# Modulation products of two k tiles at once in the first layer, with zero products ahead of them and the growth of the Fourier input moved ahead of both

## The chip, the cores and the metric

One core of a Trainium2 chip runs the whole program. The metric is the device time of one execution in microseconds; lower is better. The engines named below are TensorE (PE in the rows; PEld is its weight load), VectorE (DVE), ScalarE (ACT), GpSimd (POOL) and SyncE (SP), which issues most of the loads.

## The reference, cut to what matters

Two layers of an encoder over two requests with shared weights (512 and 256 tokens, width 1024). What matters here is the beginning of the first layer:

```
mod = silu(c) @ w_ada[l] + b_ada[l]                 # c: one row for each request
sh1, sc1, gt1, sh2, sc2, gt2 = split(mod, 6)        # 1024 columns each
h = rms_norm(x, g_mix_pre[l]) * (1 + sc1) + sh1     # 768 tokens x 1024
z = h @ w_in[l]                                     # u_f is 512 of its columns (Fourier branch)
```

The modulation shift `sh1` and scale `sc1` need 2 x 1024 columns of `w_ada[0]`, 8 MB. Until one tile of 128 of these columns is known, the same 128 columns of `h` can't be formed, and `h @ w_in` can't use them. All of it is float32 in effect: `h` and the weights of `w_in` are split into a high and a low part, and each product of the two is three matmuls.

## The kernel before

The first stage of layer 0 is written by hand in `start()`. The 1024 columns of `h` are eight k tiles of 128. For each k tile there are four steps' worth of work:

- the loads `ws[k, i]`: the shift and scale columns of `w_ada[0]` that belong to tile k, two blocks of 512 KB, each loaded by two DMAs of 256 KB whose rows in HBM are 128 columns (512 bytes) long;
- `ada(k)` (line 1725): `mod_mm` multiplies them with silu(c). These are eight float32 products with 256 moving columns that use 32 columns of the array each; four of them (one for each 32-column strip) run side by side. ScalarE then copies the sums out of PSUM (line 1732);
- `fin(k)` (line 1737): tiny products with `sel` (line 1744) turn the sums into columns, VectorE adds the bias and the gain (lines 292 and 294), ScalarE makes the high part of `h` (line 1750), VectorE the low part (lines 1751 and 1753) and the reversed copies (line 685), which the symmetric Fourier transform needs;
- `grow(k)` (line 1757): twelve matmuls of 128x512 (lines 1765 to 1767) add tile k's part of `u = h @ w_in[:, fourier]` for the four token tiles of the first request. The third matmul of a token tile needs the low part; token tiles 2 and 3 read the reversed copies.

The weights of `w_in` for `grow` are `uw[0]` to `uw[3]`, each for two k tiles. `keep(n)` (line 1782) issues n products of a constant with a block of zeros, whose sums nobody reads. `norm(4)`, `norm(5)` and `h_step` (lines 1700 and 433) bring in the second request: its two token tiles are normalized, transposed (line 398) and scaled. After `grow(7)` come the steps `us[2]`, the same growth for the second request (lines 770 to 772).

The order of the work: steps are a list, and `run()` emits them one by one. Up to step 43 (`FIXED`, which is `grow(6)` in both versions) every engine does its instructions in the order in which they are written; behind that a scheduler decides. Before a step is emitted, `run()` issues the loads that come next, as far as the step's `hold` allows (five loaded blocks not yet used, here), so SP's queue has the loads in the order in which the steps need them. A load waits until its block is free and until the eighth load before it has landed.

Before the change the steps interleave: `fin(k + 1)`, `ada(k + 2)`, `grow(k)`. So while VectorE and ScalarE work on `fin(k + 1)`, TensorE has `ada(k + 2)` and `grow(k)` to do.

Of the kernel before, what the change touches and what calls it, by code (L numbers as in the profile page):

```python
# [11 lines left out]
F32 = mybir.dt.float32  # L12
F32R = mybir.dt.float32r
AF = mybir.ActivationFunctionType
# [3 lines left out]
D = 1024  # L18
# [23 lines left out]

HP = 50
FIXED = 43
KEEP = [0, 0, 0, 2, 3, 0]
SPIN = [17, 14]


# [19 lines left out]
def encoder_trunk(ctx, tc, a, consts, y_prompt, y_sample):  # L68
    nc = tc.nc
# [11 lines left out]
    def nm(s):  # L81
        uid[0] += 1
        return f"{s}_{uid[0]}"

    def row(dt=F32):
        return rp.tile([128, 768], dt, tag="r", name=nm("r"))

    def double(dt=F32, shape=(128, 1536)):
        return dbl.tile(list(shape), dt, tag="d", name=nm("d"))
# [8 lines left out]
    def blk(dt=F32, shape=(128, 1024)):  # L98
        blocks.append(wp.tile(list(shape), dt, tag="w", name=nm("w")))
        return blocks[-1]  # L100
# [6 lines left out]
    def small(n=2):  # L107
        return sp.tile([128, n], F32, tag=f"s{n}", name=nm("s"))

    def bank():  # L110
        return pp.tile([128, 512], F32, tag="ps", name=nm("ps"))

    def f(ap):
        return ap.bitcast(F32)
# [6 lines left out]
    sel = cp.tile([128, 2], F32, name="sel")  # L121
# [85 lines left out]
    def rstd(sums, n=1):  # L207

        v, r = small(1), small(1)
        if len(sums) > 1:  # L210
            nc.gpsimd.tensor_scalar(out=v, in0=sums[0], scalar1=EPS, scalar2=sums[1], op0=ALU.add, op1=ALU.add)
        else:
            nc.gpsimd.tensor_scalar(out=v, in0=sums[0], scalar1=1.0 / n, scalar2=EPS, op0=ALU.mult, op1=ALU.add)
        nc.gpsimd.tensor_tensor(out=r, in0=v, in1=neg_half, op=ALU.pow)
        return r

    def mean_square(out, x, n, acc):
        nc.scalar.activation(out=out, in_=x, func=AF.Square, scale=float(n) ** -0.5, accum_out=acc)  # L218
# [56 lines left out]
    def mod_mm(ps, srcs):  # L275

        for s in range(2):
            for j in range(4):
                k = s * 4 + j
                nc.tensor.matmul(ps[32 * j:32 * j + 32, :], c32[:, k, :], srcs[k], start=(s == 0), stop=(s == 1),  # L280
                                 tile_position=(0, 32 * j))
# [1408 lines left out]
    def start(uw, us, S):  # L1690

        out = []
        mp, pu, xl, xT = {}, [], {}, []
        ws = {}
        for k in range(8):
            for i in range(2):
                parts = [(s * 512, 512, a["w_ada"][0][i * 512:(i + 1) * 512, s * D + k * 128:s * D + (k + 1) * 128].rearrange(
                    "(j p) c -> p j c", p=128), ("p (j c) -> p j c", dict(j=4))) for s in range(2)]
                ws[k, i] = Weight(parts, 1024, split=False)

        def norm(t):
            def emit():
                x = xl.pop(t)
                jk, ss = blk(F32), small(1)
                mean_square(jk, x, D, ss)
                nc.vector.tensor_scalar_mul(out=x, in0=x, scalar1=rstd([ss]))
                if t >= 4:
                    state["xn", t] = lambda k: x[:, k * 128:k * 128 + 128]
                    return
                if t == 0:  # L1710
                    xT.extend(bank() for _ in range(8))
                for k in range(8):
                    nc.tensor.transpose(xT[k][:, t * 128:(t + 1) * 128], x[:, k * 128:(k + 1) * 128], ident)
                for k in range(8) if t == 3 else []:
                    if k % 2 == 0:
                        d = double()
                    r = d[:, (k % 2) * 512:(k % 2) * 512 + 512]
                    if k % 2:
                        nc.vector.tensor_copy(out=r, in_=xT[k])
                    else:  # L1720
                        nc.scalar.activation(out=r, in_=xT[k], func=AF.Copy)
                    xT[k] = r
            return Step(emit, 0)

        def ada(k):
            def emit():
                ps = bank()
                mod_mm(ps[:, 0:256].rearrange("p (s c) -> p s c", s=2),
                       [ws[k, j // 4].raw.rearrange("p (s j c) -> p j s c", s=2, j=4)[:, j % 4] for j in range(8)])
                ws[k, 0].raw = ws[k, 1].raw = None  # L1730
                m = row(F32)
                nc.scalar.activation(out=m[:, 0:256], in_=ps[:, 0:256], func=AF.Copy)
                mp[k] = m
            early = [] if k % 2 else [uw[k // 2]]
            return Step(emit, 0.9, early + [ws[k, 0], ws[k, 1]], hold=5)

        def fin(k):
            def emit():
                if k == 0:
                    state["H"] = new_h()  # L1740
                m = mp.pop(k)
                p2 = bank()
                for s in range(2):
                    nc.tensor.matmul(p2[:, 2 * s:2 * s + 2], m[:, s * 128:(s + 1) * 128], sel, start=True, stop=True)
                for s in range(2):
                    mod_vec(0, s, "sc" if s else "sh", k, 1, p2[:, 2 * s:2 * s + 2].rearrange("p (k r) -> p k r", r=2))
                sc, sh = state["sc", 0, 1][:, k, 0:1], state["sh", 0, 0][:, k, 0:1]
                hi, lo = state["H"][k]
                d, x = xT[k], xT[k][:, 0:512]
                nc.scalar.activation(out=hi[:, 0:512], in_=x, func=AF.Identity, scale=sc, bias=sh)  # L1750
                nc.vector.scalar_tensor_tensor(out=x, in0=x, scalar=sc, in1=f(hi[:, 0:512]), op0=ALU.mult,
                                               op1=ALU.subtract)
                nc.vector.tensor_scalar_add(out=lo[:, 0:512], in0=x, scalar1=sh)
                xT[k] = None
                reverse(k)
            return Step(emit, 0.3, hold=5)

        def grow(k):
            def emit():
                if k == 0:  # L1760
                    pu.extend(bank() for _ in range(4))
                vh, vl = view(uw[k // 2], 2)
                for t in range(4):
                    hi, lo = u_lhs(k, t)
                    nc.tensor.matmul(pu[t], hi, vh[:, k % 2], start=(k == 0), stop=False)
                    nc.tensor.matmul(pu[t], hi, vl[:, k % 2], start=False, stop=False)
                    nc.tensor.matmul(pu[t], lo, vh[:, k % 2], start=False, stop=(k == 7))
                if k == 7:
                    u_out(S["U", 0], 0, pu[0:2])
                    u_out(S["U", 0], 1, pu[2:4])  # L1770
                    pu.clear()
            return Step(emit, 12 * 512 * MM_US, hold=5)

        def loads():
            for t in range(4):
                xl[t] = load_x(x_in[t])
                if t == 1:
                    v0.emit()
            load_tables()

        def keep(n):

            def emit():
                if not n:
                    return
                ps = bank()
                for _ in range(n):
                    nc.tensor.matmul(ps[0:32, 0:256], c32[:, 0, :], zeros, start=True, stop=True)
            return Step(emit, 0)

        zeros = cp.tile([128, 256], F32, name="zeros")
        nc.vector.memset(zeros, 0.0)
        K = KEEP
        out += [Step(loads, 0), keep(K[0]), Step(make_c, 0), keep(K[1])]
        for t in range(4):
            out += [norm(t), keep(K[2])]
        out += [ada(0), f0, keep(K[3]), fin(0), keep(K[4]), ada(1), keep(K[5])]
        for st in out:
            st.hold = 4
        out[0].hold = out[1].hold = -1  # L1800
        out += [fin(1), grow(0), ada(2)]
        for k in range(1, 8):
            out += [fin(k + 1)] if k < 7 else []
            out += [ada(k + 2)] if k < 6 else []
            out += {2: [Step(lambda: xl.update({4: load_x(x_in[4])}), 0)], 3: [Step(lambda: xl.update({5: load_x(x_in[5])}), 0)],
                    4: [norm(4)], 5: [norm(5)], 6: [h_step(("sc", 0, 1), ("sh", 0, 0), 2)]}.get(k, [])
            out.append(grow(k))
        for st in out[18:]:
            st.hold = 5
        return out + [v1] + us[2] + [f1]  # L1810
# [71 lines left out]
```

## Time and profile before

| what | value |
|---|---|
| median of 3 runs | 2285.0 us (2283.81 to 2285.89) |
| the profiled execution | 2284.37 us, span 2282.6 us |
| mean granted TensorE clock | 0.992 |
| TensorE busy in the span | 2248.0 us (98%) |
| VectorE, ScalarE busy | 1673.1 us (73%), 1307.1 us (57%) |
| DMA, mean over the span | 116 GB/s |

The span runs from the first to the last instruction; 1.8 us of the profiled execution lie outside it. TensorE is busy nearly all the time, so what the change does to the time has to be read from what TensorE does in the stretch that changes: the first 60 us. The granted clock is 1.00 at 2.4 GHz and 0.50 at 1.2 GHz.

### The profile page before, as it was taken

How to read it: one execution, taken by the hardware profiler on the slowest of the kernel's cores; microseconds unless marked ns; L12 is line 12 of the kernel's file. 1: busy time of each engine (PE TensorE's matmuls, PEld its weight loads, DVE VectorE, ACT ScalarE, POOL GpSimd, SP SyncE). 2: the span in 40 equal slices, each digit the busy share in tenths (PEclk: the TensorE clock that was granted, in tenths of full speed). 3: DMA queues.
4: the chain of work that ended last, by engine and by line, in shares of the span. 5: the costliest groups of instructions: out<-in, count | busy, mean ns of one | idle time of the engine just before them, and what ended most of it. 6: DMA issues, size and time to landing. Idle time of an engine off the chain costs nothing. (4 is left out here: it accounts for less than half of the span.)

```text
span 2282.6 us, 33282 instructions
## 1 busy us (share of the span) xinstructions
PE 2248.0 (98%) x12582; PEld 2034.4 (89%) x12582; DVE 1673.1 (73%) x2744; ACT 1307.1 (57%) x2434; POOL 177.1 (8%) x313
## 2 busy tenths in 40 slices
PE   7999999999999999999999999999999999999998
PEld 5899889988889989999989988899888999999997
DVE  5976957774587887787798688677636887666677
ACT  4545425552566777777565543455416577777773
POOL 1001300000110000000030032000001000000001
PEclk9999999999999999999999999999999899999999
DMA  9355741143322333342344575312423232212223
GB/s 280 103 167 210 215 125 36 49 142 124 121 84 73 119 111 102 93 125 79 120 139 125 164 255 153 110 35 75 166 98 109 84 111 77 81 56 74 65 74 130
DMA packets 243805, 265.89 MB, mean 116 GB/s; under 512 B 20604, under 2 KB 193318, under 8 KB 243645
## 3 DMA queue, kind: packets, MB, share of 16 engines
q1 hardware_dynamic: 235885, 235.85, 33.3%
q0 software_dynamic: 7760, 27.92, 3.6%
q8 instruction: 99, 1.62, 0.3%
q14 instruction: 61, 0.50, 0.1%
HBM read 225.89 MB, written 31.54 MB: 113 GB/s over the span
## 5 line engine op out<-in xcount | busy, mean ns | idle before, releaser
L575 PE MATMUL ps<-d,w 128*128 128x384 f32 (+2 forms) x1680 | 563.0, 335 | 8.7 <-ACT ps L601 4.5
L576 PE MATMUL ps<-d,w 128*128 128x384 f32 (+2 forms) x1680 | 561.8, 334 | 0.0
L577 PE MATMUL ps<-d,w 128*128 128x384 f32 (+2 forms) x1680 | 561.2, 334 | 0.4 <-DVE w L522 0.3
L522 DVE TENSOR_TENSOR w<-w,w 128x512 fp32r<-128x512 f32 x406 | 272.0, 686 | 102.0 <-ACT w L521 98.9
L575 PEld LDWEIGHTS ps<-d,w 128*128 128x128 f32 x1680 | 321.0, 191 | 24.4 <-ACT ps L601 5.9
L576 PEld LDWEIGHTS ps<-d,w 128*128 128x128 f32 x1680 | 321.1, 191 | 9.4
L577 PEld LDWEIGHTS ps<-d,w 128*128 128x128 f32 x1680 | 320.9, 191 | 2.2 <-DVE w L522 1.8
L521 ACT ACTIVATE w<-w 128x512 fp32r<-128x512 f32 x406 | 248.3, 626 | 72.4 <-PE ps L577 25.4
L190 PE MATMUL ps<-d,w 128*128 128x512 f32 x704 | 241.3, 344 | 1.1 <-DVE w L197 1.1
L191 PE MATMUL ps<-d,w 128*128 128x512 f32 x704 | 221.5, 337 | 0.0
L161 ACT ACTIVATE w<-w 128x1024 fp32r<-128x1024 f32 (+4 forms) x140 | 141.4, 1016 | 77.9 <-PE ps L193 26.0
L322 DVE SCALAR_TENSOR_TENSOR w<-w,c,w 128x1024 f32<-128x1024 f32 x140 | 175.5, 1277 | 13.5 <-DMA w<-in_w_ada_dram 13.3
L162 DVE TENSOR_TENSOR w<-w,w 128x1024 fp32r<-128x1024 f32 (+4 forms) x140 | 162.6, 1168 | 30.3 <-ACT w L161 13.9
L193 PE MATMUL ps<-d,w 128*128 128x512 f32 x704 | 181.9, 338 | 0.0
L1532 ACT ACTIVATE w<-ps 128x512 f32<-128x512 f32 x216 | 127.4, 590 | 86.5 <-PE ps L1530 85.6
L1530 PE MATMUL ps<-w,d 128*128 128x512 f32 x432 | 171.3, 397 | 0.0
L1529 PE MATMUL ps<-w,d 128*128 128x512 f32 x432 | 170.5, 395 | 0.0
L1527 PE MATMUL ps<-w,d 128*128 128x512 f32 x432 | 167.6, 389 | 0.0
L190 PEld LDWEIGHTS ps<-d,w 128*128 128x128 f32 x704 | 132.1, 188 | 33.2 <-DVE r L896 2.0
L191 PEld LDWEIGHTS ps<-d,w 128*128 128x128 f32 x704 | 132.4, 188 | 15.8 <-DVE d L197 0.6
L636 DVE TENSOR_TENSOR r<-ps,r 128x384 f32<-128x384 f32 (+2 forms) x92 | 49.3, 537 | 105.0 <-PE ps L577 105.0
L1440 DVE SCALAR_TENSOR_TENSOR r<-r,v,r 128x511 f32<-128x511 f32 (+1 forms) x176 | 100.6, 613 | 34.2 <-ACT r L1437 33.9
(271 smaller groups left out, 4401.9 us busy)
## 6 DMA issues: line engine op xcount, KB each, us to landing
w<-in_w_up_dram SPq DMA_DIRECT2D x88, 512.0 KB, 3.9
w<-in_w_ada_dram SPq DMA_DIRECT2D x80, 512.0 KB, 3.8
w<-in_w_in_dram SPq DMA_DIRECT2D x48, 512.0 KB, 6.7
w<-in_w_down_dram SPq DMA_DIRECT2D x72, 256.0 KB, 3.0
xs<-w SPq DMA_DIRECT2D x18, 512.0 KB, 2.7
w<-xs SPq DMA_DIRECT2D x18, 512.0 KB, 3.4
w<-in_w_ada_dram SPq DMA_DIRECT2D x32, 256.0 KB, 5.8
w<-in_w_attn_o_dram SPq DMA_DIRECT2D x16, 512.0 KB, 3.6
```

What stands on the lines that cost most here:

```text
L190: nc.tensor.matmul(o, lh, rh[:, c0:c0 + s], start=(first and k == 0), stop=False)
L191: nc.tensor.matmul(o, lh, rl[:, c0:c0 + s], start=False, stop=False)
L193: nc.tensor.matmul(o, ll, rh[:, c0:c0 + s], start=False, stop=(last and k == n - 1))
L322: nc.vector.scalar_tensor_tensor(out=box[r], in0=x, scalar=c, in1=box[r], op0=ALU.mult, op1=ALU.add)
L521: nc.scalar.activation(out=us[i].hi, in_=z, func=AF.Copy)
L522: nc.vector.tensor_sub(out=us[i].lo, in0=z, in1=f(us[i].hi))
L575: nc.tensor.matmul(ps, wh[:, k], x, start=(start and k == 0), stop=False, skip_group_check=True)
L576: nc.tensor.matmul(ps, wh[:, k], y, start=False, stop=False, skip_group_check=True)
L577: nc.tensor.matmul(ps, wl[:, k], x, start=False, stop=(k == 3), skip_group_check=True)
L1527: nc.tensor.matmul(ps, gh[:, cc], dc.hi[:, o], start=(c == 0 and j == js[0]), stop=False, skip_group_check=True)
L1529: nc.tensor.matmul(ps, gh[:, cc], dc.lo[:, o], start=False, stop=False, skip_group_check=True)
L1530: nc.tensor.matmul(ps, gl[:, cc], dc.hi[:, o], start=False, stop=(j == js[-1]), skip_group_check=True)
```

## The change

For k tiles 0 and 1 nothing changes. From the third tile on, two tiles are taken together:

- the weights: `ws[k, i]` for k = 2, 4, 6 are four blocks, with the columns of tiles k and k + 1 side by side. The rows in HBM are 256 columns (1024 bytes) long; the number of loads and their bytes are the same (24 loads of 256 KB);
- `ada2(k)` takes the place of `ada(k)` and `ada(k + 1)`: eight products with 512 moving columns, and one copy by ScalarE. `fin(k)` and `fin(k + 1)` each take their half of the row;
- `keep(16)` stands ahead of `ada2(2)`, and `keep(8)` ahead of `ada2(4)` and of `ada2(6)`: 32 zero products that were not there;
- the steps' order: `grow(1)`, `grow(3)` and `grow(5)` now stand ahead of the zero products and of `ada2(2)`, `ada2(4)` and `ada2(6)`, and the two `fin` steps stand right behind `ada2`. `ada2`'s own `hold` of 6 is set to 5 again by the loop at the end, as for its neighbours.

So the steps now read: `grow(0)`, `grow(1)`, `keep(16)`, `ada2(2)`, `fin(2)`, `fin(3)`, `grow(2)`, `grow(3)`, `keep(8)`, `ada2(4)`, `fin(4)`, `fin(5)`, `grow(4)`, `grow(5)`, `keep(8)`, `ada2(6)`, `fin(6)`, `norm(5)`, `fin(7)`, `h_step`, `grow(6)`, `grow(7)`.

```
--- before.py
+++ after.py
@@ -42,7 +42,7 @@
 
 HP = 50
 FIXED = 43
-KEEP = [0, 0, 0, 2, 3, 0]
+KEEP = [0, 0, 0, 2, 3, 0, 16, 8]
 SPIN = [17, 14]
 
 
@@ -1692,10 +1692,15 @@
         out = []
         mp, pu, xl, xT = {}, [], {}, []
         ws = {}
-        for k in range(8):
+        for k in range(2):
             for i in range(2):
                 parts = [(s * 512, 512, a["w_ada"][0][i * 512:(i + 1) * 512, s * D + k * 128:s * D + (k + 1) * 128].rearrange(
                     "(j p) c -> p j c", p=128), ("p (j c) -> p j c", dict(j=4))) for s in range(2)]
+                ws[k, i] = Weight(parts, 1024, split=False)
+        for k in range(2, 8, 2):
+            for i in range(4):
+                parts = [(s * 512, 512, a["w_ada"][0][i * 256:(i + 1) * 256, s * D + k * 128:s * D + (k + 2) * 128].rearrange(
+                    "(j p) c -> p j c", p=128), ("p (j c) -> p j c", dict(j=2))) for s in range(2)]
                 ws[k, i] = Weight(parts, 1024, split=False)
 
         def norm(t):
@@ -1722,6 +1727,18 @@
                     xT[k] = r
             return Step(emit, 0)
 
+        def ada2(k):
+
+            def emit():
+                ps = bank()
+                mod_mm(ps.rearrange("p (s c) -> p s c", s=2),
+                       [ws[k, j // 2].raw.rearrange("p (s j c) -> p j s c", s=2, j=2)[:, j % 2] for j in range(8)])
+                for i in range(4):
+                    ws[k, i].raw = None
+                m = mp[k] = mp[k + 1] = row(F32)
+                nc.scalar.activation(out=m[:, 0:512], in_=ps, func=AF.Copy)
+            return Step(emit, 1.8, [uw[k // 2]] + [ws[k, i] for i in range(4)], hold=6)
+
         def ada(k):
             def emit():
                 ps = bank()
@@ -1739,9 +1756,10 @@
                 if k == 0:
                     state["H"] = new_h()
                 m = mp.pop(k)
+                n, c = (256, k % 2 * 128) if k > 1 else (128, 0)
                 p2 = bank()
                 for s in range(2):
-                    nc.tensor.matmul(p2[:, 2 * s:2 * s + 2], m[:, s * 128:(s + 1) * 128], sel, start=True, stop=True)
+                    nc.tensor.matmul(p2[:, 2 * s:2 * s + 2], m[:, s * n + c:s * n + c + 128], sel, start=True, stop=True)
                 for s in range(2):
                     mod_vec(0, s, "sc" if s else "sh", k, 1, p2[:, 2 * s:2 * s + 2].rearrange("p (k r) -> p k r", r=2))
                 sc, sh = state["sc", 0, 1][:, k, 0:1], state["sh", 0, 0][:, k, 0:1]
@@ -1798,13 +1816,17 @@
         for st in out:
             st.hold = 4
         out[0].hold = out[1].hold = -1
-        out += [fin(1), grow(0), ada(2)]
+        out += [fin(1), grow(0)]
         for k in range(1, 8):
+            if k == 1:
+                out += [grow(1), keep(KEEP[6]), ada2(2), fin(2)]
+                continue
+            out += [grow(k)] if k in (3, 5) else []
+            out += [keep(KEEP[7]), ada2(k + 1)] if k in (3, 5) else []
             out += [fin(k + 1)] if k < 7 else []
-            out += [ada(k + 2)] if k < 6 else []
             out += {2: [Step(lambda: xl.update({4: load_x(x_in[4])}), 0)], 3: [Step(lambda: xl.update({5: load_x(x_in[5])}), 0)],
                     4: [norm(4)], 5: [norm(5)], 6: [h_step(("sc", 0, 1), ("sh", 0, 0), 2)]}.get(k, [])
-            out.append(grow(k))
+            out += [grow(k)] if k not in (3, 5) else []
         for st in out[18:]:
             st.hold = 5
         return out + [v1] + us[2] + [f1]
```

**TensorE behind grow(0).** First the order before: the last row of `grow(0)`, then `ada(2)`, `fin(1 + 1)`, `ada(3)`, and the first row of `grow(1)` (`zeros` is `keep`'s, `sel` is `fin`'s, `c` is silu(c); x4 merges four products of one block).

```order
L1767 MATMUL ps_327<-w_234,w_282 128x512
L280 MATMUL ps_352<-w_243,c_88 32x256 x4
L280 MATMUL ps_352<-w_291,c_88 32x256 x4
L1744 MATMUL ps_363<-sel,r_361 128x2 x2
L280 MATMUL ps_383<-w_294,c_88 32x256 x4
L280 MATMUL ps_383<-w_308,c_88 32x256 x4
L1765 MATMUL ps_324<-w_234,d_263 128x512
```

Now the order after the change: the last row of `grow(1)`, which follows `grow(0)` without anything between them, then `keep(16)`, `ada2(2)`, `fin(2)`, `fin(3)` and the first token tile of `grow(2)`. In the new file the growth's lines are 1783 to 1785, `fin`'s is 1762 and `keep`'s 1806.

```order
L1785 MATMUL ps_327<-w_234,w_282 128x512
L1806 MATMUL ps_352<-zeros,c_88 32x256 x16
L280 MATMUL ps_387<-w_243,c_88 32x512 x2
L280 MATMUL ps_387<-w_291,c_88 32x512 x2
L280 MATMUL ps_387<-w_294,c_88 32x512 x2
L280 MATMUL ps_387<-w_308,c_88 32x512 x2
L1762 MATMUL ps_398<-sel,r_396 128x2 x2
L1762 MATMUL ps_412<-sel,r_396 128x2 x2
L1783 MATMUL ps_324<-w_369,d_265 128x512
L1784 MATMUL ps_324<-w_370,d_265 128x512
L1785 MATMUL ps_324<-w_369,d_266 128x512
```

What moved: between `fin(2)` and the growth of tile 2 there was a whole growth of another tile and an `ada`; now there is only `fin(3)`.

**ScalarE at the same place.** Before, the copies out of PSUM (L1732) and the high parts of `h` (L1750) alternate, one of each for a tile; L161 is the high part of a `w_in` block.

```order
L161 ACTIVATE w_340<-w_241 128x1024
L1732 ACTIVATE r_361<-ps_352 128x256
L1750 ACTIVATE d_265<-d_225,m_274,m_276 128x512
L1732 ACTIVATE r_392<-ps_383 128x256
L1750 ACTIVATE d_265<-d_225,m_274,m_276 128x512
L161 ACTIVATE w_419<-w_344 128x1024
```

After, one wider copy (L1739) stands ahead of the high parts of two tiles (L1768).

```order
L161 ACTIVATE w_369<-w_241 128x1024
L1739 ACTIVATE r_396<-ps_387 128x512
L1768 ACTIVATE d_265<-d_225,m_274,m_276 128x512 x2
L161 ACTIVATE w_460<-w_373 128x1024
```

What moved: the high part of tile 2 now waits for the products of tile 3 as well, since both come out in one copy.

**TensorE at the third pair.** After the change, from the last row of `grow(5)` to the first transposes of `h_step` (L398).

```order
L1785 MATMUL ps_327<-w_460,w_498 128x512
L1806 MATMUL ps_550<-zeros,c_88 32x256 x8
L280 MATMUL ps_565<-w_466,c_88 32x512 x2
L280 MATMUL ps_565<-w_469,c_88 32x512 x2
L280 MATMUL ps_565<-w_472,c_88 32x512 x2
L280 MATMUL ps_565<-w_475,c_88 32x512 x2
L1762 MATMUL ps_582<-sel,r_574 128x2 x2
L1762 MATMUL ps_604<-sel,r_574 128x2 x2
L398 MATMUL ps_617<-ident,w_425 128x128
L398 MATMUL ps_617<-ident,w_503 128x128
```

What moved: before, `fin(7)` and the transposes followed `grow(5)` directly; now the zero products, the last `ada2` and both `fin` steps lie between. On VectorE the normalization of the sixth token tile (`norm(5)`) stands behind `fin(6)` and ahead of `fin(7)` in both versions. Behind the stage, every engine has the same instructions in the same order as before.

On SP's queue the loads of the last two pairs keep their order, except that the first half of the second request's x (`w_425` in the rows above) is now issued ahead of `uw[3]` and not two tiles later. All loads for `ada2(6)` and those behind it wait for blocks that earlier steps free.

## Rows read from the trace of the kernel before

**Rows 1.** The page's first line.

```profile
span 2282.6 us, 33282 instructions
```

**Rows 2.** Waits of TensorE from 60 us on: total, times, longest; first and last.

```profile
PE ps L575 <- ACT ps L601: 4.5, 6, 1.1
...
PE ps L577 <- DVE w L522: 0.3, 1, 0.3
```

**Rows 3.** Windows: busy us of PE, PEld, DVE, ACT, POOL; clock, DMA share, GB/s.

```profile
24.90:28.90 4.00, 2.62 (x37) 1.28 (x36) 2.17 (x7) 1.20 (x2) 0.29 (x2) 1.00 1.13 321
28.90:32.30 3.40, 3.40 (x15) 2.45 (x8) 1.25 (x4) 0.39 (x1) 0.18 (x1) 0.50 1.16 296
48.10:54.30 6.20, 5.09 (x35) 4.36 (x32) 3.54 (x13) 3.33 (x7) 1.29 (x5) 1.00 1.06 274
59.90:91.00 31.10, 30.40 (x160) 25.99 (x158) 30.81 (x50) 15.85 (x28) 0.64 (x1) 1.00 0.20 64
```

**Rows 4.** Timeline of TensorE, zero products: start us, us, engine, line, shapes, count.

```profile
17.14 1.05 PE L1788 MATMUL ps<-zeros,c 128*32 128x256 f32 x4
...
18.66 1.27 PE L1788 MATMUL ps<-zeros,c 128*32 128x256 f32 x5
```

**Rows 5.** Timeline from 24.9 us: ada(2), fin(2), ada(3), in order of time.

```profile
24.92 1.07 PE L280 MATMUL ps<-w,c 128*32 128x256 f32 x16
...
26.06 0.38 ACT L1732 ACTIVATE r<-ps 128x256 f32<-128x256 f32 x1 [1.67 <-PE ps L280]
...
26.50 0.61 PE L1744 MATMUL ps<-sel,r 128*128 128x2 f32 x4 [0.50 <-ACT r L1732]
...
27.14 0.23 DVE L292 TENSOR_TENSOR m<-ps,v 128x2 f32<-128x2 f32 x2 [0.85 <-PE ps L1744]
...
27.66 0.81 ACT L1750 ACTIVATE d<-d,m,m 128x512 fp32r<-128x512 f32 x1 [1.21 <-DVE m L294]
...
28.55 0.79 PE L280 MATMUL ps<-w,c 128*32 128x256 f32 x8 [0.88 <-DMA w<-in_w_ada_dram]
...
29.29 0.49 DVE L1753 TENSOR_SCALAR d<-d,m 128x512 fp32r<-128x512 f32 x1
...
29.69 0.49 DVE L685 CAST w<-d 128x255 fp32r<-128x255 f32 x2
```

**Rows 6.** The page's groups: a ScalarE copy of 512 columns from PSUM, elsewhere in the kernel.

```profile
L1532 ACT ACTIVATE w<-ps 128x512 f32<-128x512 f32 x216 | 127.4, 590 | 86.5 <-PE ps L1530 85.6
```

**Rows 7.** Timeline from norm(5) to the first product behind grow(7).

```profile
49.64 1.05 ACT L218 ACTIVATE w<-w 128x1024 f32<-128x1024 f32 x1
...
51.97 0.75 DVE L1706 TENSOR_SCALAR w<-w,s 128x1024 f32<-128x1024 f32 x1 [0.79 <-POOL s L214]
...
52.78 1.86 PE L398 MATMUL ps<-ident,w 128*128 128x128 f32 x15 [1.11 <-DVE w L1706]
...
54.39 0.48 PE L1765 MATMUL ps<-w,d 128*128 128x512 f32 x1
...
59.93 0.39 PE L770 MATMUL ps<-w,d 128*128 128x512 f32 x1
```

**Rows 8.** Timeline: first product of grow(1), and the first instruction behind its twelve.

```profile
29.27 0.79 PE L1765 MATMUL ps<-w,d 128*128 128x512 f32 x1
...
33.52 0.50 PE L1744 MATMUL ps<-sel,r 128*128 128x2 f32 x4
```

**Rows 9.** Timeline: VectorE's first work on the grown sums; TensorE's next wait.

```profile
61.00 1.28 DVE L714 TENSOR_TENSOR w<-w,ps 128x512 f32<-128x512 f32 x2
...
91.40 0.44 PE L575 MATMUL ps<-d,w 128*128 128x384 f32 x1 [1.09 <-ACT ps L601]
```

**Rows 10.** Loads: eight issues in a row; the last ada's wait; GB/s, 1.5 us slices from 0.

```profile
16.19 7.64 SPq L150 DMA_DIRECT2D w<-in_w_ada_dram  x8
...
47.55 0.16 PEld L280 LDWEIGHTS ps<-w,c 128*32 128x32 f32 x8 [0.47 <-DMA w<-in_w_ada_dram]
...
GB/s 0 273 194 320 310 305 287 324 326 290 291 291 349 318 290 291 290 300 353 305 295 297 269 301 333 316 304 356 323 295 338 328 299 285 268 273 47 29 31 16
```

More of the change, by code (lines that the diff above doesn't have):

```diff
@@ L44 @@
 FIXED = 43
-KEEP = [0, 0, 0, 2, 3, 0]
+KEEP = [0, 0, 0, 2, 3, 0, 16, 8]
 SPIN = [17, 14]
@@ L1694, in start @@
         ws = {}
-        for k in range(8):
+        for k in range(2):
             for i in range(2):
@@ L1698, in start @@
                     "(j p) c -> p j c", p=128), ("p (j c) -> p j c", dict(j=4))) for s in range(2)]
+                ws[k, i] = Weight(parts, 1024, split=False)
+        for k in range(2, 8, 2):
+            for i in range(4):
+                parts = [(s * 512, 512, a["w_ada"][0][i * 256:(i + 1) * 256, s * D + k * 128:s * D + (k + 2) * 128].rearrange(
+                    "(j p) c -> p j c", p=128), ("p (j c) -> p j c", dict(j=2))) for s in range(2)]
                 ws[k, i] = Weight(parts, 1024, split=False)
@@ L1723, in norm, with ada2, emit @@
             return Step(emit, 0)
+        def ada2(k):
+            def emit():
+                ps = bank()
+                mod_mm(ps.rearrange("p (s c) -> p s c", s=2),
+                       [ws[k, j // 2].raw.rearrange("p (s j c) -> p j s c", s=2, j=2)[:, j % 2] for j in range(8)])
+                for i in range(4):
+                    ws[k, i].raw = None
+                m = mp[k] = mp[k + 1] = row(F32)
+                nc.scalar.activation(out=m[:, 0:512], in_=ps, func=AF.Copy)
+            return Step(emit, 1.8, [uw[k // 2]] + [ws[k, i] for i in range(4)], hold=6)
         def ada(k):
@@ L1741, in emit @@
                 m = mp.pop(k)
+                n, c = (256, k % 2 * 128) if k > 1 else (128, 0)
                 p2 = bank()
                 for s in range(2):
-                    nc.tensor.matmul(p2[:, 2 * s:2 * s + 2], m[:, s * 128:(s + 1) * 128], sel, start=True, stop=True)
+                    nc.tensor.matmul(p2[:, 2 * s:2 * s + 2], m[:, s * n + c:s * n + c + 128], sel, start=True, stop=True)
                 for s in range(2):
@@ L1800, in start @@
         out[0].hold = out[1].hold = -1
-        out += [fin(1), grow(0), ada(2)]
+        out += [fin(1), grow(0)]
         for k in range(1, 8):
+            if k == 1:
+                out += [grow(1), keep(KEEP[6]), ada2(2), fin(2)]
+                continue
+            out += [grow(k)] if k in (3, 5) else []
+            out += [keep(KEEP[7]), ada2(k + 1)] if k in (3, 5) else []
             out += [fin(k + 1)] if k < 7 else []
-            out += [ada(k + 2)] if k < 6 else []
             out += {2: [Step(lambda: xl.update({4: load_x(x_in[4])}), 0)], 3: [Step(lambda: xl.update({5: load_x(x_in[5])}), 0)],
                     4: [norm(4)], 5: [norm(5)], 6: [h_step(("sc", 0, 1), ("sh", 0, 0), 2)]}.get(k, [])
-            out.append(grow(k))
+            out += [grow(k)] if k not in (3, 5) else []
         for st in out[18:]:
```

## The prediction

> **What bounds the kernel now.** I began with the page's head and the waits of TensorE. The span is 2282.6 us [rows 1] and TensorE is busy for 98% of it. From 60 us on its waits are for ScalarE or VectorE alone, ten rows from 4.5 us in six times down to 0.3 us once; none is for a load [rows 2]. ScalarE and VectorE in turn live on what TensorE makes, so whatever delays TensorE in the first 60 us moves the rest of the program with it, unless one of those waits gives a part back. The question is therefore one number: when does the first product behind `grow(7)` start? Before, that is 59.93 us [rows 7].
>
> The windows show what the stretch up to there is like [rows 3]. The DMA engines are full (share 1.13 and 1.16 up to 32.3 us, 1.06 up to 54.3 us), but TensorE is nearly full as well. It waits for a load 0.88 us at 28.55 us [rows 5], and between 28.9 and 32.3 us its granted clock is 0.50, that is 1.2 GHz. From 48.1 to 54.3 us it is busy 5.09 us of 6.20 at the full clock. So there is little waiting that new TensorE work could fill.
>
> **The zero products.** One `keep(2)` is four matmuls in the trace, so a float32 product is two passes [rows 4]. Five passes take 1.27 us, four 1.05 us: 0.22 us for a pass, 0.44 us for a product. TensorE takes its matmuls in order, so 16 products cost 7.0 us, eight cost 3.5 us, and all 32 cost 14.1 us wherever TensorE would not have waited. Would it have waited? The loads for tiles 2 and 3 had landed by 28.55 us, when the second half of `ada(3)` ran [rows 5], and the very last `ada` found its loads at 47.55 us, after 0.47 us in which the weight load waited [rows 10]. The loads keep their number, size and order, but for one earlier 512 KB load of x. The new order comes to the three `ada2` at about 35, 50 and 64 us (below), at least 6 us, some 2 us and 16 us after these times. The second of these is a bound only, since 47.55 us is the landing of a later load. Loads of the third pair wait for blocks that `ada2(2)` frees at 36.7 us; 3 MB at some 300 GB/s [rows 10] is 10 us, 47 us, still well ahead of 64 us. So I take the zero products at their full price.
>
> **The products of two tiles.** `ada` is busy 1.07 us: four passes of 0.22 us one behind the other on each strip, and 0.19 us to drain [rows 5]. With 512 columns the passes double: 1.95 us for two tiles, against 2 x 1.07 us. ScalarE's copy starts 0.07 us behind the products (24.92 + 1.07 = 25.99, 26.06) and takes 0.59 us for 512 columns [rows 6] in place of 0.38 us; there are three copies in place of six.
>
> **What is late behind them.** Count from the end of an `ada2`. The copy ends at 0.66, `fin` starts at 0.72. In the rows of `fin(2)` [rows 5] the high part ends 1.97 us after `fin`'s start (27.66 + 0.81 - 26.50), the low part after 3.28 us (29.29 + 0.49 - 26.50), the last reversed copy after 3.68 us. So the first growth product of the pair can start at 2.7 us, its third product, which needs the low part, at 4.0 us. Before, an `ada` and a whole growth covered this; now only the second `fin` does, about 0.5 us. A growth product takes 0.231 us ((59.93 - 54.39) / 24) [rows 7], so the first growth runs two products, waits 0.8 us, and ends ten products after 4.0, at 6.3 us. VectorE begins the second `fin` at 4.4 us and has its low part 2.64 us later (29.29 + 0.49 - 27.14), at 7.05 us; the second growth waits 0.25 us and ends at 9.4 us.
>
> The third pair has the transposes of `h_step` behind it, and these need `norm(5)`. Its ScalarE part can start when the high part of tile 6 is done, at 2.7 us; VectorE's part follows 2.33 us later (51.97 - 49.64), the transposes 0.81 us after that, the growth 1.61 us after them [rows 7]: 7.45 us. 24 growth products of 0.231 us end it at 13.0 us.
>
> **The sum.** `grow(0)` ends where `ada(2)` begins now, 24.92 us. `grow(1)` follows at once, its inputs being ready: 27.7. `keep(16)`: 34.7. `ada2(2)`: 36.7. The pair: 46.1. `keep(8)` and `ada2(4)`: 51.6. The pair: 61.0. `keep(8)` and `ada2(6)`: 66.4. The last part: 79.4 us, against 59.93: **19.5 us later**. Of these, 14.1 us are the zero products; the other 5.4 us are the uncovered chains, less the waits that vanish.
>
> **The clock.** In the 4.0 us behind the end of an `ada2` TensorE would stand idle for about 2.5 us. The window from 24.9 to 28.9 us has 1.38 us idle, and 0.50 of the clock follows; the one from 48.1 to 54.3 us has 1.11 us idle and keeps 1.00 [rows 3]. A growth at the low clock took 4.25 us [rows 8], against 12 x 0.231 = 2.77: 1.5 us lost. The change avoids that one stretch (already in the sum, since `grow(1)` stands at full speed) and opens three gaps larger than the one that led to it. Between none and three (0 to 4.5 us) I take two, 3.0 us. The Trainium skill (TensorE: Matmul & The Clock Gate, "HAM oscillation — how this bites in real kernels") tells of a loop that waits for data in each turn: the clock fell at every one of the waits, and the loss was half of the time spent at the low clock. By that rule all three gaps would cost half of a stretch of 3.4 us [rows 3], 5.1 us in all, and the result would be 2.1 us above mine. The trace agrees that the clock falls behind a gap, with a loss of 1.5 us.
>
> **What is given back.** VectorE starts on the grown sums 1.07 us after `grow(7)` (61.00 against 59.93), is then busy 30.81 of 31.10 us [rows 3], and TensorE waits 1.09 us at 91.40 us for the work in its wake [rows 9]. If TensorE is late by more than VectorE, as behind a slow clock, up to 1.1 us comes back; I take it whole. Without it the forecast is 1.1 us higher.
>
> 19.5 + 3.0 - 1.1 = 21.4 us on the profiled execution of 2284.4 us: **2305.8 us**. Its own time is 0.6 us under the median of the runs, which I leave out. A measurement of this kernel can tell about 0.2%, 4.6 us, from no change.
>
> **Rivals.**
> - *The zeros don't hold the clock.* They use 32 of the array's 128 columns, and the longest run in the trace is five passes [rows 4], so a run of 7 us at full clock isn't shown. If half of them run at 1.2 GHz, 14.1 us becomes 21.2: 2313 us; all of them, 2320 us. Against it, the five passes at 18.66 us keep the pace of the four at 17.14. Chance 0.08.
> - *A part of the zeros lies in waits for loads.* For the first pair this needs landings after 34.7 us, 6 us later than before; the second pair is the closer one. With all three runs covered, 21.4 - 14.1 = 7.3 us are left: 2292 us. For it speaks the full DMA share. Chance 0.07 for 2290 to 2299 us.
> - *No change that can be told:* zeros covered, and the chains shorter than in the rows, by half of the 5.4 us: about 2287 us. Chance 0.03.
> - *The transfers set the end, and the change shortens them.* This is the faster one. If the arrival of the loads, not TensorE's work, decides when `grow(7)` ends, then rows of 1024 bytes help. The 24 loads take 0.955 us each (7.64 / 8) [rows 10], 22.9 us; from the usual 300 GB/s to the best slice's 356, they would be 3.6 us shorter. With the waits of 0.88 us [rows 5] and 1.11 us [rows 7] and the 1.5 us of low clock gone: 2284.4 - 7.1 = 2277 us. It decides only if the pairs' loads land later than the zero products end. Against it stands TensorE's own work from 24.92 us: eight growths less one (19.4 us), the zeros, three `ada2` (5.9), six `fin` (3) and the transposes (1.6) are 44 us, where 35 us were used. Chance 0.03. The Trainium skill (DMA: Bandwidth & Descriptors, "Why small descriptors are slow (HBM only)") gives a fixed 3 cycles for each packet beside one for each 32 bytes; an estimate from it is 35 cycles for 1024 bytes against 2 x 19, 8% or 1.8 us in place of the 3.6. No run so far shows such rows.
>
> **Range and chances.** The forecast has 0.79: from 2299 us (no low clock, waits 3 us shorter in all) to 2313 us (three low stretches, nothing back, and 3 us of longer waits or zeros at the low clock). Outside lie the covered zeros, the two cases below, and the far end of the first rival, together some 0.2. Slower by over 0.2%: 0.79 + 0.08 + 0.07 = 0.94; within 0.03; faster 0.03.
>
> **What the changed profile would show.** The first product of lines 770 to 772 near 80 us. The group of zero products with 64 matmuls more than the ten of before, each run without an idle gap on either side, 7.0 us and twice 3.5 us long. No wait of `ada2` for a load. TensorE waiting for ScalarE's high part (two to three times about 1 us and more) and for VectorE's low part ahead of a third growth product. A clock of 0.50 in a stretch behind two or three of the `ada2`. From there to the end the same rows as before, later by one constant. I would be wrong if `ada2` waits for a DMA behind the zeros, if the zero passes are shorter than 0.22 us or run beside other work, or if waits of the later program shrink by more than the 1.1 us.

## The result, and the profile after

| what | before | after |
|---|---|---|
| median of the runs | 2284.40 us (4 runs, 2283.32 to 2285.89) | 2311.89 us (4 runs, 2310.80 to 2312.41) |
| ratio to before | | 1.0118, 95% interval 1.0106 to 1.0130 |
| the profiled execution | 2284.37 us | 2310.80 us |
| mean granted clock | 0.992 | 0.989 |

The changed kernel is slower by 27.5 us between the medians and by 26.4 us between the profiled executions, of which the span has 26.1. The forecast was 21.4.

```profile
span 2308.7 us, 33310 instructions
```

The span of before is in [rows 1]. TensorE has 16 matmuls more: 64 zero passes came, 48 passes of `ada` went.

I read TensorE's timeline of the changed stretch first. Columns: start us, us, engine, line, operation, tiles, shapes, count, and in brackets the idle time ahead and what ended it.

```profile
24.49 0.39 PE L1783 MATMUL ps<-w,d 128*128 128x512 f32 x1
...
27.30 6.88 PE L1806 MATMUL ps<-zeros,c 128*32 128x256 f32 x31
...
34.23 1.88 PE L280 MATMUL ps<-w,c 128*32 128x512 f32 x13
36.88 1.05 PE L1762 MATMUL ps<-sel,r 128*128 128x2 f32 x8 [0.76 <-ACT r L1739]
38.90 0.50 PE L1783 MATMUL ps<-w,d 128*128 128x512 f32 x1 [0.97 <-ACT d L1768]
...
40.22 0.50 PE L1785 MATMUL ps<-w,d 128*128 128x512 f32 x1 [0.58 <-DVE d L1771]
```

The zero products (L1806) stand between the last `grow(1)` product and `ada2(2)` (L280) with no idle time on either side. Then come three waits: 0.76 us for the copy of both tiles (L1739), where the copy of one tile cost 0.50 [rows 5], 0.97 us for the high part (L1768) and 0.58 us for the low part (L1771), which [rows 5] didn't have in this place. The second pair repeats the first two of them, the third pair the first:

```profile
53.16 1.05 PE L1762 MATMUL ps<-sel,r 128*128 128x2 f32 x8 [0.76 <-ACT r L1739]
55.19 0.80 PE L1783 MATMUL ps<-w,d 128*128 128x512 f32 x1 [0.97 <-ACT d L1768]
...
64.14 3.42 PE L1806 MATMUL ps<-zeros,c 128*32 128x256 f32 x15
...
75.46 3.44 PE L398 MATMUL ps<-ident,w 128*128 128x128 f32 x15 [4.01 <-DVE w L1711]
78.57 0.55 PE L1783 MATMUL ps<-w,d 128*128 128x512 f32 x1
...
84.22 0.39 PE L770 MATMUL ps<-w,d 128*128 128x512 f32 x1
```

In the third pair the transposes (L398) wait 4.01 us for `norm(5)` (L1711), where they waited 1.11 us before [rows 7]. The first product behind `grow(7)` starts at 84.22 us against 59.93: 24.3 us later.

The waits of TensorE from 14 to 84 us (total, times, longest), without one of 0.52 us for the copy of `fin(1)`, which was there before:

```profile
PE ps L398 <- DVE w L1711: 4.0, 1, 4.0
PE ps L1762 <- ACT r L1739: 2.3, 3, 0.8
PE ps L1783 <- ACT d L1768: 1.9, 2, 1.0
PE ps L280 <- DMA w<-in_w_ada_dram: 0.8, 1, 0.8
PE ps L1785 <- DVE d L1771: 0.6, 1, 0.6
```

The one wait for a load is that of `ada(0)`, at 15.95 us, which the change doesn't touch. No `ada2` waits for one.

Now the same stretch by windows (busy us of PE, PEld, DVE, ACT, POOL; granted clock, DMA share, GB/s):

```profile
27.30:34.20 6.90, 6.90 (x36) 3.59 (x39) 0.00 (x0) 0.00 (x0) 0.00 (x0) 1.00 1.08 364
36.30:41.20 4.90, 2.77 (x14) 2.12 (x15) 2.32 (x10) 1.61 (x3) 0.37 (x2) 1.00 1.10 353
41.20:44.60 3.40, 3.40 (x9) 2.64 (x9) 2.78 (x5) 1.49 (x2) 0.37 (x2) 0.50 0.33 125
...
54.80:61.70 6.90, 6.42 (x14) 4.63 (x15) 4.75 (x13) 3.14 (x5) 1.47 (x6) 0.51 0.90 225
...
71.90:78.70 6.80, 3.24 (x16) 3.25 (x16) 4.73 (x13) 3.92 (x8) 1.47 (x6) 0.50 0.00 0
```

Zero products run almost alone from 27.3 to 34.2 us, and the clock is 1.00 (2.4 GHz). Behind each `ada2` TensorE has idle time, 2.1 us of 4.9 behind the first, and a stretch at 0.50 (1.2 GHz) follows or overlaps: 3.4 us, 6.9 us and 6.8 us long. In the last one TensorE is busy for 3.24 us only.

From 84 us on, the rows that answer [rows 9], and the window that answers the last of [rows 3]:

```profile
83.80 1.38 DVE L714 TENSOR_TENSOR w<-w,ps 128x512 f32<-128x512 f32 x2
```

```profile
112.30 0.60 ACT L877 ACTIVATE r<-ps 128x512 f32<-128x512 f32 x1 [3.90 <-PE ps L193]
112.80 1.66 ACT L437 ACTIVATE d<-w 128x512 fp32r<-128x512 f32 x3
...
114.25 0.34 PE L597 MATMUL ps<-w 128*128 128x384 f32 x1
114.36 0.62 ACT L521 ACTIVATE w<-w 128x512 fp32r<-128x512 f32 x1
114.88 0.37 ACT L878 ACTIVATE r<-ps 128x256 f32<-128x256 f32 x1
115.14 0.49 ACT L601 ACTIVATE ps<-ps 128x384 f32<-128x384 f32 x1
...
115.69 0.44 PE L575 MATMUL ps<-d,w 128*128 128x384 f32 x1 [1.10 <-ACT ps L601]
```

```profile
83.80:115.30 31.50, 30.79 (x162) 26.35 (x160) 30.00 (x47) 14.39 (x26) 0.64 (x1) 1.00 0.20 63
```

TensorE's wait is as long as before, 1.10 us against 1.09, and comes 24.29 us later. The rows ahead of it show what fills it: a product of TensorE (L193) releases ScalarE at 112.30 us, and from there ScalarE does seven instructions without a pause, of which the last one (L601) makes what L575 needs. TensorE comes to that place behind L597, while ScalarE still has three of the seven to finish. To follow the rest I set each matmul from the first L770 on against the same one of before. The lateness is 24.3 us up to 130 us of the old time, 24.5 at 600, 25.9 at 700, 27.0 at 1300 and 26.1 at the end.

### The profile page after: what moved, and what is told of

The parts are those of the page before. It is cut to its first block, busy times and chain, and to the rows that moved or that the text cites. A ratio compares the mean times of both kernels' runs of the same rounds, so it can differ in the third digit from the quotient of the medians.

```text
span 2308.7 us, 33310 instructions
## 1 busy us (share of the span) xinstructions
PE 2267.6 (98%) x12598; PEld 2044.6 (89%) x12598; DVE 1673.6 (72%) x2744; ACT 1306.4 (57%) x2431; POOL 180.1 (8%) x313
## 5 line engine op out<-in xcount | busy, mean ns | idle before, releaser
L575 PE MATMUL ps<-d,w 128*128 128x384 f32 (+2 forms) x1680 | 563.3, 335 | 9.8 <-ACT ps L601 4.9
L577 PE MATMUL ps<-d,w 128*128 128x384 f32 (+2 forms) x1680 | 561.2, 334 | 0.4 <-DVE w L522 0.3
L522 DVE TENSOR_TENSOR w<-w,w 128x512 fp32r<-128x512 f32 x406 | 271.9, 686 | 101.1 <-ACT w L521 98.1
L575 PEld LDWEIGHTS ps<-d,w 128*128 128x128 f32 x1680 | 320.9, 191 | 26.3 <-ACT ps L601 6.4
L577 PEld LDWEIGHTS ps<-d,w 128*128 128x128 f32 x1680 | 321.1, 191 | 2.1 <-DVE w L522 1.8
L521 ACT ACTIVATE w<-w 128x512 fp32r<-128x512 f32 x406 | 248.3, 626 | 73.4 <-PE ps L577 25.9
L322 DVE SCALAR_TENSOR_TENSOR w<-w,c,w 128x1024 f32<-128x1024 f32 x140 | 175.5, 1277 | 14.3 <-DMA w<-in_w_ada_dram 14.2
L161 ACT ACTIVATE w<-w 128x1024 fp32r<-128x1024 f32 (+4 forms) x140 | 141.2, 1016 | 76.3 <-PE ps L193 26.0
L193 PE MATMUL ps<-d,w 128*128 128x512 f32 x704 | 181.9, 338 | 0.0
```

Of the source, the lines that this page charges most:

```text
L193: nc.tensor.matmul(o, ll, rh[:, c0:c0 + s], start=False, stop=(last and k == n - 1))
L322: nc.vector.scalar_tensor_tensor(out=box[r], in0=x, scalar=c, in1=box[r], op0=ALU.mult, op1=ALU.add)
L521: nc.scalar.activation(out=us[i].hi, in_=z, func=AF.Copy)
L522: nc.vector.tensor_sub(out=us[i].lo, in0=z, in1=f(us[i].hi))
L575: nc.tensor.matmul(ps, wh[:, k], x, start=(start and k == 0), stop=False, skip_group_check=True)
L577: nc.tensor.matmul(ps, wl[:, k], x, start=False, stop=(k == 3), skip_group_check=True)
```

## Experiments

All of them compute the whole result.

**The change without its zero products.** The new order and the wide pair stay.

```
-KEEP = [0, 0, 0, 2, 3, 0, 16, 8]
+KEEP = [0, 0, 0, 2, 3, 0, 0, 0]
```

> The changed kernel without its 32 new zero products (the counts ahead of the three ada2 set to 0); order and weights as changed. Theory A (the zeros stand at full price, since the loads had landed before them): the first product of us[2] moves from 84.2 us to about 70 us, three gaps behind the ada2 stay, and the time falls by 13 to 15 us, to 2297 to 2299 us. Rival B (the zeros hold the clock up or stand where TensorE would wait for loads anyway): ada2 then waits for loads or the low clock lasts longer, and at most 7 us come back: 2305 us or more.

Measured: 2297.72 us, 1.0054 of before (1.0039 to 1.0069), so 14.2 us less than the changed kernel by medians. The first L770 product came at 71.14 us, 13.1 us earlier. Here `grow(1)` ended at 28.10 us and not at 27.30; counted from its end the step is 13.9 us. What remained are the same waits:

```profile
PE ps L398 <- DVE w L1711: 4.0, 1, 4.0
PE ps L1762 <- ACT r L1739: 2.2, 3, 0.7
PE ps L1783 <- ACT d L1768: 1.9, 2, 1.0
PE ps L1785 <- DVE d L1771: 0.6, 1, 0.6
```

With the zeros gone no wait for a load took their place. So they had covered nothing, and the 14.1 us of the sum were real, as expected.

**The zero products alone, in the kernel before.**

```
-FIXED = 43
+FIXED = 46
...
         for k in range(1, 8):
             out += [fin(k + 1)] if k < 7 else []
+            out += [keep(16 if k == 1 else 8)] if k in (1, 3, 5) else []
             out += [ada(k + 2)] if k < 6 else []
```

(`FIXED` counts the three new steps, so it is `grow(6)` still.)

> The kernel before with nothing changed but the zero products: 16 ahead of ada(3), 8 ahead of ada(5) and 8 ahead of ada(7). Theory A: 14.1 us of new work, less the 0.9 us wait for a load and the 1.5 us of low clock that it covers, so 10 to 13 us slower than before, 2295 to 2298 us. Rival B (they lie in waits): within 5 us of before.

Measured: 2297.10 us, 1.0052 (1.0037 to 1.0067); the first L770 product at 70.88 us, 10.9 us later than before. Its window from `ada(2)`'s old place to there:

```profile
24.90:70.88 45.98, 45.48 (x291) 31.04 (x289) 22.28 (x60) 16.18 (x30) 4.60 (x19) 1.00 0.75 205
```

TensorE is busy for all but 0.5 us and the clock is 1.00 throughout. Here the waits of 0.88 us [rows 5] and 1.11 us [rows 7] and the 1.5 us of low clock are gone, 3.5 us. `ada(2)` also starts 1.3 us later than in the trace of before, at 26.18 us, so that 13.7 us of zeros less 3.5 and 1.3 more make 11.5, against 10.9. That the zeros took the place of the two waits is seen; that they kept the low clock away isn't shown, since the second trace of the kernel before, further down, has none in this stretch either.

**The new order alone**, with before's narrow loads and products and without zeros.

```
-        out += [fin(1), grow(0), ada(2)]
+        out += [fin(1), grow(0)]
         for k in range(1, 8):
+            if k == 1:
+                out += [grow(1), ada(2), ada(3), fin(2)]
+                continue
+            out += [grow(k), ada(k + 1), ada(k + 2)] if k in (3, 5) else []
             out += [fin(k + 1)] if k < 7 else []
-            out += [ada(k + 2)] if k < 6 else []
...
-            out.append(grow(k))
+            out += [grow(k)] if k not in (3, 5) else []
```

> The kernel before with the order alone: grow(1), grow(3), grow(5) ahead, then the ada of two tiles one behind the other with the old narrow weights, then the two fin; no zero products. Theory A: the uncovered chains and the low clock behind them are the order's doing: 10 to 15 us slower than before, 2295 to 2300 us, with TensorE waiting for ScalarE's high part and for norm(5) as in the changed kernel. Rival C (the two-tile weights are what costs, since nothing can start before four blocks have landed): the order alone costs under 4 us.

Measured: 2292.68 us, 1.0034 (1.0021 to 1.0047), 7.3 us slower; the first L770 product at 66.14 us, 6.2 us later. The waits from 24 to 84 us:

```profile
PE ps L398 <- DVE w L1706: 3.9, 1, 3.9
PE ps L1765 <- ACT d L1750: 1.7, 2, 0.8
PE ps L1767 <- DVE d L1753: 1.2, 2, 0.6
```

The waits for the copy are missing: with two products the first tile's sums are out before the second tile's products end. The order accounts for some 7 us, less than the 10 to 15 expected and more than the rival's 4: neither held. The wide pair adds 5 us to that (71.14 against 66.14), of which 1.9 us are waits (8.7 against 6.8 in the two lists). It also has 10.2 us more at the low clock (17.1 us against 6.8, by the windows at 0.50); the next run got 5.2 us back for the 17.1, so an estimate for the 10.2 is 3.1 us, which is the rest.

**The clock's part.** The change without its blocks of zeros, but with a few zero products in the gaps behind `ada2`. They run while TensorE would wait.

```
-                out += [grow(1), keep(KEEP[6]), ada2(2), fin(2)]
+                out += [grow(1), ada2(2), keep(1), fin(2)]
...
-            out += [keep(KEEP[7]), ada2(k + 1)] if k in (3, 5) else []
+            out += [ada2(k + 1), keep(1)] if k in (3, 5) else []
             out += [fin(k + 1)] if k < 7 else []
+            out += [keep(8 if k == 6 else 2)] if k in (2, 4, 6) else []
```

(`FIXED` is 46 here too.)

> The changed kernel with 15 zero products in other places: none ahead of the ada2; one between each ada2 and its first fin, two behind the second fin of the first two pairs, eight ahead of the transposes of the third. Theory A: they fit into the gaps in which TensorE stands idle anyway, so against the kernel without new zeros they cost at most 1 us, and if the clock then stays at 1.00 they gain 3 to 5 us: about 2293 to 2295 us. Rival D (products on 32 columns do not hold the clock): clock and time as without zeros, 2297 to 2300 us.

Measured: 2295.04 us, 1.0041 (1.0027 to 1.0056). The first L770 product came at 66.62 us, 4.5 us earlier than without any zeros, and 5.2 us earlier counted from the first `ada2`, which starts at 28.77 us here and at 28.10 there. By windows:

```profile
24.00:66.60 42.60, 40.13 (x212) 25.74 (x211) 22.31 (x61) 16.85 (x28) 4.28 (x19) 1.00 0.71 221
66.60:99.90 33.30, 31.11 (x163) 26.39 (x161) 32.28 (x52) 16.96 (x29) 1.19 (x2) 1.00 0.23 72
99.90:103.30 3.40, 3.40 (x11) 3.40 (x12) 3.40 (x7) 1.26 (x2) 0.00 (x0) 0.50 0.72 177
```

The low clock is gone from the whole stage, so it had cost about 5 us there. Of the 4.5 us only 2.7 were left at the end, a little less than the 3 to 5 expected. They were given back where TensorE first catches up with VectorE:

```profile
99.80 0.62 PE L577 MATMUL ps<-d,w 128*128 128x384 f32 x1 [1.09 <-DVE w L522]
```

That wait is 0.31 us long in the changed kernel; here it is 1.09, and the stretch at 0.50 stands right behind it.

**The transposes' wait.** `norm(5)` ahead of the last zeros and `ada2(6)`; all else as changed.

```
+            out += [norm(5)] if k == 5 else []
...
-                    4: [norm(4)], 5: [norm(5)], 6: [h_step(("sc", 0, 1), ("sh", 0, 0), 2)]}.get(k, [])
+                    4: [norm(4)], 6: [h_step(("sc", 0, 1), ("sh", 0, 0), 2)]}.get(k, [])
```

> The changed kernel, zero products and all, with norm(5) put ahead of the last zero products and of ada2(6), where its input has long landed (second load of x issued at 37.7 us). Theory A (the third gap of 4.0 us and the transposes at low clock behind it come from norm(5), which can start only when ScalarE is done with the high part of tile 6): the transposes follow fin(7) at once, grow(6) waits about 0.6 us for its low part, and 4 to 5.5 us come back: 2306 to 2308 us. Rival E (the transposes merely swap one wait for another, on the low parts of tiles 6 and 7): under 2 us come back, 2310 us or more.

Measured: 2314.20 us, 1.0128 (1.0112 to 1.0143): 2.3 us slower than the changed kernel, and the expectation failed. In the stage it did nearly as expected: the first transposes didn't wait, the last four of them waited 1.49 us for `fin(7)`, and the first L770 product came at 80.52 us, 3.7 us earlier. Matmul against matmul that lead holds up to 110 us and is down to 0.5 at 116. The two long waits of TensorE between 84 and 130 us:

```profile
PE ps L577 <- DVE w L522: 3.0, 1, 3.0
PE ps L575 <- ACT w L521: 1.6, 1, 1.6
```

and what follows them:

```profile
116.10:122.00 5.90, 5.90 (x18) 5.90 (x19) 4.29 (x7) 2.27 (x4) 0.00 (x0) 0.50 0.56 157
```

These two waits have 3.2 us more than the 1.4 us of the changed kernel in this place. The stretch at the low clock behind them, matmul against matmul, takes another 2.4 us. On VectorE the work on the grown sums (L714) starts at 81.89 us against 83.80, 1.9 us earlier and not 3.7, and between it and the L522 that TensorE waits for the scheduler has put 50 instructions in place of 47. So here VectorE set the pace, and the lead of TensorE bought nothing. Since the order behind the stage isn't the same, the run doesn't test the lead by itself.

**The kernel before, profiled again**, to see how far two executions of one program drift apart.

> The kernel before once more, unchanged, for a second trace of it. If the 1 to 2 us that every changed kernel loses behind the first 60 us (at 645 to 665 us, and 1250 to 1290 us) vary between executions, this trace shows a part of them against the first trace; if they belong to the changes, it lies within 0.3 us of the first trace everywhere behind 60 us.

Measured: 2283.79 us (one run), span 2282.0. Against the first trace its matmuls are 0.06 us late from 60 up to 130 us, 0.5 at 600, 0.2 at 1300 and 0.6 early at the end. So a part of the drift lies between executions. The stage itself went another way to the same end: `ada(2)` started at 26.20 us, 1.3 us later, the clock was 1.00 from there to 60 us, and TensorE waited 0.95 us at 34.42 and 0.34 us at 47.95 for loads. The low stretch at 28.9 us [rows 3] thus belongs to one execution. That the arrival of the loads evened out the later start is likely, but was not tried.

**The wide pair, interleaved.** The wide loads and `ada2` stay, but work of another tile stands behind each `ada2`, as before the change.

```
+        out += [fin(1), grow(0), keep(4), ada2(2), grow(1), fin(2), fin(3), ada2(4), lx[0], lx[1], grow(2), fin(4), grow(3), fin(5),
+                ada2(6), grow(4), fin(6), norm(4), grow(5), norm(5), fin(7),
+                h_step(("sc", 0, 1), ("sh", 0, 0), 2), grow(6), grow(7)]
```

(This stands in place of the loop over k. `lx` are the two loads of the second request's x; `FIXED` is 41, `grow(6)` again.)

> The two-tile weights and ada2 of the changed kernel, in an order that again covers every fin: ada2(4) between fin(3) and grow(2), fin(4) between grow(2) and grow(3), ada2(6) between fin(5) and grow(4), and so on; both loads of x behind the weights of ada2(6), four zero products in the wait ahead of ada2(2) and no others. Theory A (the loss is the zeros and the uncovered chains; the wider rows themselves shorten the loads, 353 against some 300 GB/s up to 42 us): us[2] starts 1 to 4 us earlier than before, 2281 to 2285 us, same as before within what can be told, and 27 us below the changed kernel. Rival C (two-tile weights are what costs): ada2(2) and ada2(6) wait for four blocks, the clock falls, and it is 3 us or more slower than before.

Measured: 2290.50 us (11 runs), 1.0020 (1.0012 to 1.0029). The first L770 product came at 61.58 us, the clock was 1.00 from 25 to 61.6 us, and the transposes waited 1.54 and 1.07 us for `norm(4)` and `norm(5)`. Neither expectation held: it is 4.9 us slower than before, as the rival had it, but without the rival's low clock and with only 0.4 us of waiting for a load. At the first L770 product it is 1.7 us late, behind it a wait of 1.02 us for VectorE (L577) follows at 94.62 us, and where the rest comes from was not tried.

**The same with the two normalizations a step earlier.**

```
-                ada2(6), grow(4), fin(6), norm(4), grow(5), norm(5), fin(7),
+                ada2(6), norm(4), grow(4), fin(6), norm(5), grow(5), fin(7),
```

> The interleaved order with the wide pair, and the two normalizations one step earlier: norm(4) ahead of grow(4) and fin(6), norm(5) ahead of grow(5). In the interleaved run the transposes waited 1.54 and 1.07 us for norm(4) and norm(5), and the first product behind grow(7) came at 61.58 us. Theory: the first of the two waits goes and the second falls to about 1 us, as in the kernel before; the first product behind grow(7) comes 1.0 to 1.6 us earlier, at about 60.2 us, and the time falls by as much, to about 2289 us, 1.0015 of before. Rival: VectorE sets the pace behind 60 us, so the head's gain comes back as waits of TensorE for ScalarE or VectorE between 85 and 120 us, and the time stays at 2290.5 us, 1.002 of before.

Measured: 2287.21 us (11 runs, 2285.18 to 2290.82), 1.0012 (1.0003 to 1.0021). The waits from 24 to 62 us, and the first L770 product:

```profile
PE ps L398 <- DVE w L1711: 1.6, 1, 1.6
PE ps L280 <- DMA w<-in_w_ada_dram: 0.4, 1, 0.4
```

```profile
60.38 0.39 PE L770 MATMUL ps<-w,d 128*128 128x512 f32 x1
```

One of the two waits is gone and the other is 1.6 us, not the 1 expected; the stage is 1.2 us shorter. Here VectorE came along: the second wait behind the stage is 0.3 us where it was 1.0, and nothing was given back. So the wide pair can stand at 2.8 us over the kernel before (by medians), but no version of mine beats it.

## Why the prediction was right, and where its sizes were off

**The zero products: right.** 6.9, 3.4 and 3.4 us, 13.7 against 14.1; without them the first L770 product comes 13.1 us earlier, 13.9 from the end of `grow(1)`. At full clock on 32 columns (27.30:34.20), so the rival of zeros at half clock falls; that they lie in waits for loads falls with the list of waits.

**The loads: right in effect.** That faster transfers would set the end was the rival on the other side. The transfers did become faster, by more than I allowed: eight issues in a row took 6.61 us, the longest of three such groups, where they took 7.64 [rows 10],

```profile
30.61 6.61 SPq L150 DMA_DIRECT2D w<-in_w_ada_dram  x8
```

and the same 24 us, first before and then after, moved 308 and 357 GB/s:

```profile
17.00:41.00 24.00, 22.09 (x154) 14.79 (x155) 13.41 (x37) 8.06 (x14) 1.65 (x9) 0.93 1.14 308
```

```profile
17.00:41.00 24.00, 21.16 (x119) 12.67 (x118) 8.66 (x27) 4.48 (x8) 1.10 (x6) 1.00 1.09 357
```

But no `ada2` waited for them. The Trainium skill (DMA: Bandwidth & Descriptors, "Why small descriptors are slow (HBM only)") gave an estimate of 8% less time; by these issues it was 13%, by the windows 14%.

**The chains: right.** Copy 0.60 us (0.59 forecast), then 0.76, 0.97 and 0.58 us of waits; growth 2.7 us after the end of `ada2` (36.11 to 38.90: 2.8). The third pair's transposes wait for `norm(5)` as worked out.

**The clock: right in kind, the term mis-sized.** I took two low stretches of 1.5 us each, 3.0. All three gaps brought one, and the second and third were twice as long as the one in the trace of before. The two growths of the first pair took 8.1 us from first product to next zeros (38.90 to 47.04) where my chain gives 6.7; those of the second 8.95 (55.19 to 64.14); the transposes up to the growth 3.1 (75.46 to 78.57) instead of 1.6. That is 1.4 + 2.25 + 1.5 = 5.2 us, and the run with zeros in the gaps got as much back, counted from its first `ada2`. The rule that I weighed beside the term (the Trainium skill, TensorE: Matmul & The Clock Gate, "HAM oscillation — how this bites in real kernels") came to 5.1 us: the trace agrees that every gap counts. That the sum comes out too is luck. With the stretches as measured, 17.1 us in all, half would be 8.5; in the second the wait for the low part (0.58 us in the first) falls away, so that it costs less than its half, and the last one, in which TensorE is busy for 3.24 us, costs 1.5. The 1.5 us for a stretch was itself read from a single one, which the second trace of before doesn't have.

**The sum up to 84.22 us.** 59.93 + 19.5 + 3.0 forecast 82.4; 2.2 us more of clock, less 0.4 us because `grow(0)` ended at 24.49 and not at 24.92, make 84.2.

**The give-back: wrong.** I took 1.1 us from the wait at 91.40 us; it is still 1.10 us. The condition held: VectorE's L714 is 22.8 us later than before (83.80 against 61.00) and TensorE 24.3, so VectorE has 1.5 us more of a lead. What failed is that this wait was VectorE's doing at all. By the rows from 112.30 us it is a round trip through ScalarE that starts from TensorE's own product (L193), and it is 1.10 us long in the runs without zeros, with the zeros alone and with the order alone too, whose stages end 6 to 11 us late.

**Behind it** I forecast a constant. The lateness grows by 1.8 us, in steps near 660 and 1290 us. The other changed kernels also end 0.6 to 4 us later than their first L770 product does (with `norm(5)` early, whose waits are told above, 8.7), not in the same places, and two executions of one program differ by 0.5 us there. Two terms of this are seen. One is a wait of 0.9 us for VectorE near 1311 us in the kernel after, where it had been 0.2. The other is the clock: near 660 us a stretch at 0.50 lasts 17.1 us where it lasted 10.2, here first before and then after,

```profile
653.60:663.70 10.10, 10.10 (x42) 10.10 (x42) 10.03 (x19) 6.79 (x11) 0.00 (x0) 0.50 0.25 80
```

```profile
672.70:689.70 17.00, 16.68 (x72) 16.49 (x72) 16.24 (x29) 9.80 (x18) 0.00 (x0) 0.50 0.40 123
```

and the lateness grows by 0.9 us there; near 1780 us it is the other way round (10.2 us where it was 17.1), and the lateness falls by 0.8. The second trace of before has 13.7 and 10.2 us in the same two places, so these lengths differ between executions of one program. What brings them and the rest about was not tried and stays open.

Together: 21.4 + 1.8 for the clock and the start + 1.1 for the give-back + 1.8 later = 26.1 us, of 26.4 measured in the profiled executions. By the medians of the run without zeros (12.4 us over before) and of that with the order alone (7.3), the 27.5 us split into some 15 for the zeros, 5 for the wide pair and 7 for the order.

## What to carry to other kernels

Zero products cost their full time ahead of work that is ready. Here 15 of them in the gaps, where the engine would stand still, kept the clock up, and 32 ahead of the gaps didn't. When one instruction is widened to serve two steps, ask what the first step now waits for, and keep another tile's work behind it. A lead of one engine can be lost at the next wait for another, as in two runs here: look at the next wait behind the stage before counting a saving.

## What I had not expected

- With rows of 1024 bytes for most of the loads, 357 GB/s moved from 17 to 41 us; with rows of 512 bytes and loads of the same size, 308.
- In the run with zeros in the gaps two waits of 1.09 us, at 98.08 and 99.80 us, stand ahead of a stretch at the low clock. In the run of the zeros alone the same two waits, 1.10 us each at 102.34 and 104.06 us, are followed by none. What tells the two apart was not tried.
- One normalization moved by one step changed what the scheduler puts between two instructions of VectorE behind the stage, and that run lost more there than it had gained in the stage.
